# Half of one LayerNorm's transposes moved from TensorE to DMA, with the projection behind it regrouped

## The chip, the cores and the metric

The kernel runs on one core of a Trainium2 chip. The core has TensorE (PE: matrix products and, against an identity, transposes; both go to PSUM), VectorE (DVE), ScalarE (ACT), GpSimd (POOL) and a queue for transfers that SyncE (SP) issues. Each engine works off its own list of instructions in order. The metric is the device time of one execution in microseconds, the median of several.

## The reference, cut to what matters

One layer of a streaming encoder works on 256 tokens of 2048 features in float32. The part that matters here is the seam between its first feed-forward block and its mixer:

```
h = LN(alpha*h + 0.5*SwiGLU_1(h))                      # first FFN, then this LayerNorm
proj = h @ w_in                                        # one combined projection
qa, ka, va, q_lat, kv_lat, gates = split(proj)         # va: 1024 columns, gates: 4096
```

The LayerNorm takes mean and variance over the 2048 features of a token, and then a gain and a bias per feature. Two attentions, a cross attention and a second FFN follow.

## The kernel before, in words

**Operands.** Each float32 operand of a product is split into a rounded high part (hi, a copy by ACT) and the rest (lo, a subtraction by DVE). A product is three matmuls: hi by hi, lo of the activations by hi of the weights, and hi of the activations by lo of the weights. TensorE contracts over 128 features at a time, so 2048 features are 16 K tiles. Tokens come in two halves of 128 (`tt` 0 and 1).

**Weights.** Weights come from HBM in units of 2048 columns (1 MB) through three `raw` buffers, and are split into one of two `hi`/`lo` pairs or, where an item names tags, into free activation blocks. `add` appends an item (a function, the weights it needs, a count of weight pairs that are still held, a priority) to a list; `run` walks the list, loads and splits the weights of coming items as soon as a pair is free, and then calls the item. `weave` puts side steps ahead of the main items with given numbers. The order on each engine follows this program order, the priorities (SOON is 400, the default 0) and a compile-time estimate of when things are ready; `issue_after` pins one instruction behind another on its engine. `fetch` pins a weight load behind the transpose that was last sent before it in program order, and `send` pins a transposing transfer behind the last weight load; both are on SP.

**The LayerNorm.** At the end of the FFN, `out_proj` leaves 16 or fewer K tiles of its last column group as a skewed group: `skewed` first does four units for token half 0 and keeps their weights, and then the same four for token half 1. That lets the LayerNorm of half 0 run while TensorE still works on half 1. The next projection (A's values, `val`) is skewed in the same way, so that half 1 of the LayerNorm runs beside half 0 of the values. `ln_scale` makes mean and reciprocal root in a chain of small DVE operations. `ln_T` then takes quarters `q` of 512 features (4 K tiles): it normalises (DVE for even q, ACT for odd q), turns four 128x128 tiles on TensorE into one PSUM tile `at` (L421), applies gain and bias on the way out of PSUM (ACT L428 and DVE L430, in turns), and splits the result into hi (ACT L255) and lo (DVE L256) of the activations `T`. The transposes are pinned behind the matmul before them. Quarters 0 and 1 come ahead of the last of the four units of the other half, quarters 2 and 3 behind it.

**The values.** A's values are 1024 columns in two groups of 512. The first group's unit `g` holds K tiles 4g to 4g+3 of 512 columns, so all 16 K tiles are needed within the first four units (12 matmuls each and half). The second group follows with both halves together, 24 matmuls a unit. Each group takes two PSUM tiles of the pool `mm` (four buffers; the pool `at` has four, too). The four gate groups and the latent projection behind them take PSUM by turns: one pool for the plain products, the other for the products of sums (`mm_sums`), with the roles swapped from group to group. `forms_step` prepares sums of activations for these groups on DVE and ACT.

**Planes.** In other places the kernel already turns activations by DMA: `planes` copies float32 words on ACT as two planes of 16 bits (L846), `send` turns them by a transposing transfer on SP (L850), and `join` puts the words together again on ACT (L854). `turned_norm` does so with the LayerNorm behind the mixer: it normalises on DVE (L1405), sends, joins, applies gain and bias (ACT L1426 and DVE L1428, in turns) and splits.

## Time and profile before

| | us |
|---|---|
| median of three runs | 2433.39 (2433.3 to 2434.96) |
| profiled execution, its own time | 2432.52 |
| its span, first to last instruction | 2430.7 |
| TensorE busy in the span | 2422.3 |
| VectorE busy | 2130.9 |
| ScalarE busy | 1553.2 |

TensorE's granted clock is 1.0 throughout. The span is what lies between the first and the last instruction; the profiled execution's own time is 1.8 us more, and is 0.9 us below the median. In the views, "PE" rows are matmuls, "PEld" rows are the loads of the stationary operand, and an arrow with a name is what ended an idle time. The FFN's last matmuls lie at about 660 to 683 us of the span, the transposes of this LayerNorm between 680 and 697 us, and the values from 684 to 730 us.

### The profile page before, as it was taken

The numbers are of one execution on the slowest core, as the hardware profiler recorded it, in microseconds if no ns is written. First come the engines' busy times: TensorE is split into PE (matmuls) and PEld (weight loads), VectorE is DVE, ScalarE is ACT, GpSimd is POOL, SyncE is SP. The second block draws the span as 40 slices with busy tenths as digits, with TensorE's granted clock in tenths as the row PEclk, the third lists the DMA queues.
The fourth block names the chain that finished last, engine by engine and source line by source line (L and its number), as shares of the span: only waits on it lengthen the run. The fifth ranks groups of instructions, "written<-read, shape, count | busy, mean of one in ns | idle before, by whom it ended". The sixth has DMA issues, their size and how long they took to land.

```text
span 2430.7 us, 29702 instructions
## 1 busy us (share of the span) xinstructions
PE 2422.3 (100%) x11280; PEld 2022.8 (83%) x11280; DVE 2130.9 (88%) x2437; ACT 1553.2 (64%) x2022; POOL 35.9 (1%) x81
## 2 busy tenths in 40 slices
PE   9999999999999999999999999999999999999999
PEld 8888888888888888888888888888888888888887
DVE  8999989899889998779788889979879999888997
ACT  6676745666555557878565687765666675556662
POOL 0000000000000001000000000000000000000000
PEclk9999999999999999999999999999999999999999
DMA  7766656667656657776577577655556766666665
GB/s 268 252 212 214 207 200 222 210 201 219 224 176 215 216 195 248 229 210 176 183 246 256 167 241 213 220 181 192 190 199 214 229 221 210 220 207 207 200 220 182
DMA packets 176414, 516.20 MB, mean 212 GB/s; under 512 B 111728, under 2 KB 112496, under 8 KB 121104
## 3 DMA queue, kind: packets, MB, share of 16 engines
q1 hardware_dynamic: 170816, 495.83, 61.6%
q0 software_dynamic: 4592, 17.30, 2.2%
q8 instruction: 88, 1.44, 0.2%
q10 hardware_dynamic: 864, 1.18, 0.1%
q14 instruction: 54, 0.44, 0.1%
HBM read 485.30 MB, written 2.10 MB: 201 GB/s over the span
## 4 chain that ended last, share of the span: by engine, by line
PE 89%; DVE 4%; ACT 3%; DMA 1%; issue 1%; SPq 0%; DVEq 0%; ACTq 0%
PE at L311 24%; PE mm L311 23%; PE at L366 11%; PE mm L366 11%; PE mm L298 10%; PE mm L277 4%; PE mm L279 2%; DVE lo L267 2%; ACT hi L264 1%; PE at L1034 1%; PE at L1505 0%; PE at L277 0%; DMA raw<-w_xv 0%; PE at L1088 0%; ACT H L854 0%
## 5 line engine op out<-in xcount | busy, mean ns | idle before, releaser
L264 ACT CAST hi<-raw 128x1024 fp32r<-128x1024 f32 (+1 forms) x852 | 804.0, 981 | 458.0 <-PE at L311 150.1
L267 DVE TENSOR_TENSOR lo<-raw,hi 128x2048 fp32r<-128x2048 f32 (+1 forms) x427 | 902.0, 2114 | 134.8 <-ACT hi L264 129.0
L311 PE MATMUL mm<-hi,T 128*128 128x512 f32 (+1 forms) x1312 | 307.5, 384 | 0.8 <-DVE v L400 0.7
L311 PEld LDWEIGHTS mm<-hi,T 128*128 128x128 f32 x1312 | 244.5, 188 | 46.9 <-DVE v L400 1.1
L264 ACT CAST X<-H 128x1024 fp32r<-128x1024 f32 (+1 forms) x170 | 174.8, 1035 | 160.9 <-DVE H L248 119.9
L311 PE MATMUL at<-hi,T 128*128 128x512 f32 x1136 | 272.3, 390 | 0.0
L311 PEld LDWEIGHTS at<-hi,T 128*128 128x128 f32 x1136 | 213.3, 188 | 44.5
L267 DVE TENSOR_TENSOR X<-H,X 128x2048 fp32r<-128x2048 f32 (+1 forms) x85 | 191.4, 2252 | 64.7 <-ACT X L264 64.7
L311 PE MATMUL mm<-lo,T 128*128 128x512 f32 (+1 forms) x656 | 158.4, 383 | 0.0
L311 PE MATMUL at<-lo,T 128*128 128x512 f32 x568 | 141.0, 389 | 0.0
L311 PEld LDWEIGHTS mm<-lo,T 128*128 128x128 f32 x656 | 122.3, 188 | 22.4
L311 PE MATMUL at<-hi,H 128*128 128x512 f32 x560 | 133.8, 390 | 0.0
L311 PEld LDWEIGHTS at<-lo,T 128*128 128x128 f32 x568 | 106.7, 188 | 22.1
L311 PEld LDWEIGHTS at<-hi,H 128*128 128x128 f32 x560 | 105.0, 188 | 21.5
L250 DVE TENSOR_TENSOR H<-H,raw 128x512 f32<-128x512 f32 (+1 forms) x170 | 115.4, 679 | 2.2
L311 PE MATMUL mm<-hi,H 128*128 128x512 f32 x480 | 115.5, 392 | 0.1
L311 PEld LDWEIGHTS mm<-hi,H 128*128 128x128 f32 x480 | 89.6, 188 | 18.9 <-DVE w L684 0.5
L248 DVE TENSOR_TENSOR H<-raw 128x1024 f32<-128x1024 f32 (+1 forms) x85 | 102.1, 1201 | 0.6 <-DMA raw<-w_gate 0.4
L366 PE MATMUL mm<-X,X 128*128 128x512 f32 x342 | 91.4, 393 | 0.0
L264 ACT CAST X<-raw 128x1024 fp32r<-128x1024 f32 (+1 forms) x54 | 55.4, 1035 | 47.9 <-DVE raw L250 38.6
L366 PE MATMUL at<-X,X 128*128 128x512 f32 (+1 forms) x315 | 82.6, 386 | 0.7 <-ACT X L264 0.7
L854 ACT COPY w<-w 128x1024 uint16<-128x1024 uint16 (+1 forms) x60 | 75.7, 1275 | 1.4 <-DMA w<-w 1.4
(387 smaller groups left out, 4151.3 us busy)
## 6 DMA issues: line engine op xcount, KB each, us to landing
raw<-ffn_w_in SPq DMA_DIRECT2D x150, 1024.0 KB, 4.9
raw<-ffn_w_out SPq DMA_DIRECT2D x66, 1024.0 KB, 4.9
raw<-w_gate SPq DMA_DIRECT2D x32, 1024.0 KB, 4.8
raw<-ffn_w_out_r SPq DMA_DIRECT2D x16, 1024.0 KB, 4.9
raw<-w_qk SPq DMA_DIRECT2D x16, 1024.0 KB, 5.6
raw<-w_o_b SPq DMA_DIRECT2D x16, 1024.0 KB, 4.8
raw<-w_out SPq DMA_DIRECT2D x16, 1024.0 KB, 5.0
raw<-w_xk SPq DMA_DIRECT2D x16, 1024.0 KB, 5.4
```

Source lines behind the costliest of these rows:

```text
L248: self.nc.vector.tensor_tensor(two[0], two[1], raw[:, :m].unsqueeze(1).to_broadcast([P, 2, m]), ALU.add)
L250: self.nc.vector.tensor_tensor(t[:, a * m:a * m + m], t[:, b * m:b * m + m], raw[:, a * m:a * m + m], ALU.add)
L264: self.last_hi = self.nc.scalar.copy(hi[:, c:d], src[:, c:d])
L267: self.last_lo = self.nc.vector.tensor_tensor(lo[:, :n], src, hi[:, :n].bitcast(F32), ALU.subtract)
L277: self.nc.tensor.matmul(ps, hi[j], x.both(kt), start=(j == 0), stop=False)
L279: self.last_mm = self.nc.tensor.matmul(ps[:, :S], lo[j], x.at(0, kt), start=False, stop=(j == n - 1))
L298: self.last_mm = self.nc.tensor.matmul(ps, x.at(xi, kt)[:, tt * P:(tt + 1) * P], w[wi][:, j * 512 + c:j * 512 + c + m], start=(start and j ...
L311: self.last_mm = self.nc.tensor.matmul(ps[tt, g][:, :n], x.at(xi, kt)[:, tt * P:(tt + 1) * P], w[wi][:, c:c + n], start=first and j + wi + ...
L366: self.last_mm = self.nc.tensor.matmul(bank[:, :m], a[xi], v[wi][:, c * m:(c + 1) * m], start=own and first and wi + xi == 0, stop=own and ...
L854: self.nc.scalar.copy(self.words(u, n).rearrange("p (c k) -> p k c", k=2), self.words(s, n).rearrange("p (k c) -> p k c", k=2))
L1034: nc.tensor.matmul(ps[:, c0:c0 + nk], q[:, tt * P:(tt + 1) * P], k[:, :nk], start=(j == 0), stop=(j == len(parts) - 1))
```

## The change

Quarters 0 and 1 of this LayerNorm stay on TensorE (`near`, before the last unit of the other half, as before). Quarters 2 and 3 go by `planes`, `send` and `join`, through the blocks `F` and `X2`, for both token halves, with default priority. Their steps lie at the end of the FFN and at the items 0 to 8 of the values.

The values are read in another layout: a unit now holds one pair of K tiles of all 1024 columns (`_pairs`, `mm_pair`), so the eight units `k` go through the features in order. Units 0 to 3 (K tiles 0 to 7, quarters 0 and 1) are done by token halves, 12 matmuls each and half; units 4 to 7 (quarters 2 and 3) with both halves together, 24 each. All four PSUM tiles of `mm` are held to the end and copied out there by `values`, two by ACT and two by DVE. The gates, the latent projection and one small product behind it swap the two PSUM pools. The sums of activations for the gates keep their places in time (items 9 to 12).

```diff
-    def mm_pair(self, ps, w, n, x, kts, first, last):
+    def mm_pair(self, ps, w, n, x, kts, first, last, tts=(0, 1)):
...
-                for tt in range(2):
+                for tt in tts:
...
+    def skewed_pairs(self, src, ps, xT, side, tags):
+        kept = {}
+        def add(k, tts, tags=None, held=0, keep=False, again=False):
+            def fn(w=None):
+                if keep:
+                    kept[k] = w
+                w = kept.pop(k) if again else w
+                if k == 0:
+                    ps.update({(tt, g): self.group_tile(0) for tt in tts for g in range(2)})
+                self.mm_pair(ps, w, 512, xT(), (2 * k, 2 * k + 1), k == 0, k == 7, tts)
+            self.add(fn, *(() if again else ((src[:, k * 2048:(k + 1) * 2048], tags),)), held=held)
+        def build():
+            self.skewed(lambda tt, k, **kw: add(k, (tt,), **kw), (), tags)
+            for k in range(4, 8):
+                add(k, (0, 1))
+        self.weave(self.collect(build), side)
...
+        side = dict(steps(1))
+        for i, c in enumerate(SUMS_GATE):
+            side.setdefault(9 + i, []).append((self.forms_step(fx, SUMS_GATE, c, xT), 0))
+        side[12].insert(0, values)
+        self.skewed_pairs(t["w_va"][0], ps, xT, side, (None, None, ("H5", "H0", "early"), ("X0", "X1", "turned")))
...
-            self.pair_group(n % 2, t["w_gate"][n], 512, KT, xT, AT_GATE[n], fx, ps, qs, None, SUM_HOME + ("H5",),
+            self.pair_group(n % 2 ^ 1, t["w_gate"][n], 512, KT, xT, AT_GATE[n], fx, ps, qs, None, SUM_HOME + ("H5",),
...
-        self.pair_group(0, t["w_lat"][0], 512, KT, xT, SUMS_IN, fx, lps, lqs, None, SUM_HOME + ("H5",))
+        self.pair_group(1, t["w_lat"][0], 512, KT, xT, SUMS_IN, fx, lps, lqs, None, SUM_HOME + ("H5",))
...
-            ps = self.at_tile()
+            ps = self.mm_tile()
...
+        def near(tt):
...
+                self.ln_T(self.h[tt], got[tt], tt, ln, x["T"], (0, 1))
...
+        if not homes[0]:
+            def low(f, *a):
+                return f(*a), 0
+            side = {0: [scale(1), low(send, 0, 2), low(planes, 0, 3)], 1: [low(send, 0, 3)], 2: [low(join, 0, 2)],
+                    3: [near(1)], 4: [low(join, 0, 3), low(planes, 1, 2)], 5: [low(send, 1, 2), low(planes, 1, 3)],
+                    6: [low(send, 1, 3)], 7: [low(join, 1, 2)], 8: [low(join, 1, 3)]}
+            return lambda tt: side if tt else ([scale(0)], [near(0)], [low(planes, 0, 2)])
...
-        ln = [self.ln_steps(n, st, x) for n in ("ln_ffn1", "ln_mix", "ln_x")]
+        ln = [self.turned_norm("ln_ffn1", st, x, (None, None, "F", "X2")), None, self.ln_steps("ln_x", st, x)]
...
-    r["w_va"] = _tok(w[:, 2 * aw:3 * aw])
+    r["w_va"] = _pairs(*_halves(w[:, 2 * aw:3 * aw]), 512, [()])
```

47 lines of the change are left out of this document (16 added, 31 removed).

## The prediction

> **What bounds the kernel now.** I read the page first, then the waits of TensorE, then the seam by stages, along the chain of work, and in order of time.
>
> ```profile
> span 2430.7 us, 29702 instructions
> PE 2422.3 (100%) x11280; PEld 2022.8 (83%) x11280; DVE 2130.9 (88%) x2437; ACT 1553.2 (64%) x2022; POOL 35.9 (1%) x81
> PEclk9999999999999999999999999999999999999999
> ...
> PE at L493 <- DVE w L470: 1.1, 1, 1.1
> PE mm L311 <- DVE v L400: 0.7, 1, 0.7
> ```
>
> TensorE is busy for 2422.3 of 2430.7 us at full clock, and its longest waits for another engine are 1.1 and 0.7 us. So an edit gains only what it takes off TensorE's list, less the waits that this uncovers. The stages of the seam, each with the busy time of the engines:
>
> ```profile
> 684.04:692.52 8.48, 8.48 (x40) 6.80 (x39) 8.27 (x23) 6.09 (x11) 0.00 (x0) 1.00 0.00 0
> 692.52:696.95 4.43, 4.43 (x29) 3.87 (x28) 4.04 (x7) 3.52 (x8) 0.00 (x0) 1.00 0.48 150
> 696.95:707.93 10.98, 10.98 (x51) 9.10 (x50) 10.58 (x21) 7.21 (x12) 0.00 (x0) 1.00 0.32 109
> 707.93:729.69 21.76, 21.76 (x97) 18.02 (x96) 16.80 (x24) 10.98 (x16) 1.23 (x2) 1.00 0.61 212
> ```
>
> TensorE fills every stage. DVE is nearly full, too: 8.27 of 8.48 us and 10.58 of 10.98. ACT has 2.39, 0.91 and 3.77 us free in the first three stages, and 10.8 in the last. DMA is at 0.00 while half 0 of the values starts. The chain of work names the transposes:
>
> ```profile
> 680.29 1.04 PE at L421 x8
> ...
> 683.41 0.87 PE at L421 x8
> 684.28 8.40 PE mm L298 x36
> 692.68 0.87 PE at L421 x8
> ...
> 696.32 0.87 PE at L421 x8
> 697.20 32.66 PE mm L298 x144
> ```
>
> The four batches of eight transposes cost 1.04 us and three times 0.87. A matmul of 512 columns costs 32.66 / 144 = 0.2268 us, so a unit of 12 is 2.72 and one of 24 is 5.44.
>
> In order of time, the chain from transposes to the first value matmul, and then the second half's:
>
> ```profile
> 680.27 1.06 PE L421 MATMUL at<-ident,h 128*128 128x128 f32 x8
> 683.03 1.14 ACT L255 CAST T<-w 128x512 fp32r<-128x512 f32 x2
> 683.68 0.69 DVE L256 TENSOR_TENSOR T<-w,T 128x512 fp32r<-128x512 f32 x1 [0.34 <-ACT T L255]
> 684.04 2.28 PE L298 MATMUL mm<-hi,T 128*128 128x512 f32 x8
> 684.43 1.45 PEld L298 LDWEIGHTS mm<-hi,T 128*128 128x128 f32 x7 [0.22 <-DVE T L256]
> 690.64 1.52 ACT L415 ACTIVATE h<-h,nb,y 128x512 f32<-128x512 f32 x2 [1.90 <-DVE nb L403]
> 695.68 1.29 DVE L256 TENSOR_TENSOR T<-w,T 128x512 fp32r<-128x512 f32 x2 [0.24 <-ACT T L255]
> 696.95 2.07 PE L298 MATMUL mm<-hi,T 128*128 128x512 f32 x8
> ```
>
> This decides the first term. The transposes of half 0 start at 680.27. Quarter 0 is out of PSUM and rounded to hi from 683.03 on, and its lo ends at 683.68 + 0.69 = 684.37. The second matmul of the values reads that lo: it is the row at 684.43 with 0.22 us idle for it. TensorE already waits for the chain there, although the second batch of transposes lies between.
>
> **The change part by part.**
>
> *Transposes removed.* The second and the fourth batch go: 2 x 0.87 = -1.74 us on TensorE's list.
>
> *What comes back at half 0.* Without the second batch TensorE has its last FFN matmul out 0.87 us earlier, but the lo of quarter 0 still ends at 684.37, because the steps of that chain (transposes, four gains of each engine, hi, lo) are the same and start at the same row. The second matmul reads the lo first, in the pair layout as in the old. So +0.87: the whole batch turns into a wait. The bounds are 0, if DVE and ACT, with fewer gains to make around it, finish quarter 0 that much sooner, and 1.4, if a normalising for the planes (0.54, below) slips in front. I take 0.87, since the gains of quarters 2 and 3 lie behind this chain and not in it.
>
> *Half 1.* Three units follow, 8.2 us from the second matmul, and the transposes of half 1 stay at 692.5. After the unit of 2.72 us TensorE now arrives at 696.95 - 0.87 = 696.08, and its second matmul at 696.31. The lo of quarter 0 is the first of two in the row at 695.68, mean 0.645, so it ends between 696.33 and 696.4. That is a wait of 0.1. The bounds are 0, and 1.4 if one join's work on DVE (two gains and a lo, prices below) stands in front. I take 0.1: the near steps have the higher priority.
>
> *The detour by planes.* Four pieces (two quarters, two halves) each issue what the LayerNorm behind the mixer issues, whose rows are:
>
> ```profile
> L846 ACT COPY X<-h x4: 1038/1044/1046, 1383.9 to 1390.7; 128x1024 uint16<-128x1024 uint16 x4
> ...
> L854 ACT COPY X<-X x4: 1361/1368/1384, 1388.3 to 1407.6; 128x1024 uint16<-128x1024 uint16 x4
> ...
> L1426 ACT ACTIVATE X<-X,vecs x8: 480/504/517, 1389.7 to 1412.9; 128x128 f32<-128x128 f32 x8
> ...
> L1428 DVE TENSOR_SCALAR X<-X,vecs x8: 340/341/347, 1390.1 to 1410.3; 128x128 f32<-128x128 f32 x8
> ...
> L1405 DVE TENSOR_SCALAR h<-h,mv,y x8: 537/541/543, 1383.0 to 1393.7; 128x512 f32<-128x512 f32 x8
> ...
> L850 SPq DMA_TRANSPOSE X<-X x4: 1231/1232/3229, 1385.0 to 1391.9; - x4
> L850 SPq DMA_TRANSPOSE H<-H x12: 1231/1238/7732, 1250.0 to 1418.3; - x12
> ...
> raw<-w_va SPq DMA_DIRECT2D x8, 1024.0 KB, 5.7
> X<-X SPq DMA_TRANSPOSE x4, 4.6
> ```
>
> On ACT a piece is a planes copy 1.04, a join 1.36, two gains of 0.50 and a hi of 0.63: 4.0 us. On DVE it is a normalising 0.54, two gains of 0.34 and a lo of 0.69: 1.9. On SP it is one transfer that holds the queue for 1.23 and lands after 4.6. What it replaces, and what else stands on ACT there:
>
> ```profile
> L428 ACT ACTIVATE w<-at,vecs 128x128 f32<-128x128 f32 x16 | 6.8, 454 | 1.3 <-PE at L421 1.0
> L430 DVE TENSOR_SCALAR w<-at,vecs 128x128 f32<-128x128 f32 x16 | 6.3, 404 | 1.7 <-ACT w L428 1.6
> L255 ACT CAST T<-w 128x512 fp32r<-128x512 f32 x8 | 4.7, 619 | 0.8 <-DVE w L430 0.5
> L264 ACT CAST hi<-raw 128x1024 fp32r<-128x1024 f32 x11 | 11.1, 1052 | 9.0 <-issue 5.6 <-PE mm L298 3.4
> L891 DVE COPY H<-mm 128x512 f32<-128x512 f32 x2 | 1.4, 685 | 0.0
> L891 ACT COPY H<-mm 128x512 f32<-128x512 f32 x2 | 1.2, 577 | 0.2 <-PE mm L298 0.2
> ```
>
> Per piece ACT loses two gains of 0.45 and the hi of 0.62, and for quarter 3 a normalising of 0.8. So ACT has some 8.4 us more to do in all. DVE loses two gains of 0.40, the lo, and for quarter 2 a normalising that it does already: 0.6 more in all, which the free time of the last stage covers; without that cover it would be the 0.6. ACT's has to be followed by its deadline.
>
> The first unit that needs quarter 2 is k = 4. TensorE starts half 1 of unit 0 at 696.2, four units later it is 707.1, and the fifth matmul of unit 4 (four times 0.227 later, 708.0) is the first to read quarter 2 of half 1. From 684.2, where the two hi of quarters 0 and 1 end, ACT has in program order up to there: two hi of unit 3 (2.1), four planes (4.2), one normalising (0.8), four gains and two hi of half 1 (3.1), three pieces' joins with gains and hi (9.0), and the hi of units 4 and 5 (4.2). That is 23.3 us, so without one idle moment it ends at 707.5, and DVE's lo at 708.2, just as the sixth matmul reads it. ACT will not be free of idle: it waits in this stretch for DVE (1.90 in the row at 690.64) and for PSUM (1.0 in the L428 row). But two items on this list, the hi of unit 5 (due only at 712.5) and the planes of half 1's quarter 3, may fall behind. The bounds are 0 (these two, 3.1 us, come later) and 1.9 (worked out below). I take +0.5. The last piece is due with unit 6 at 718.0 and has ten more microseconds, with ACT half idle: nothing.
>
> *SP.* The first six loads of the values were issued by 677.6:
>
> ```profile
> 660.33 17.31 SPq L193 DMA_DIRECT2D raw<-w_va  x6
> ```
>
> Units 4 and 5 are the last two of these, and now stand behind the sends: unit 4's behind two, unit 5's behind the third, unit 6's behind the fourth. With ACT through the hi of unit 3 at 686.3, the planes end at 687.3 and 688.4, and two sends of 1.23 at 689.7; unit 4's load lands 5.7 later, at 695.4, and its buffer pair only comes free when the hi matmuls of unit 0 end, at 698. DMA stands at 0.00 before this, so that is the cover, 2.6 us wide for the start of the hi, and 10.6 for the last moment (707.1 less one cast of 1.05 and 5.7 of landing: issue by 700.3).
>
> *Values, pairs and PSUM.* 192 matmuls and eight loads of 1 MB remain; the pair order has the same forms. The four copies out of `mm` (0.58 and 0.69 each, two on either engine) come at the end. The gates start in `at`, which is free, and want `mm` only in their second unit, 5.44 us later; two copies behind one lo of 2.29 are done within 3.7. Nothing, and if that cover went, the excess over 5.44. The latent projection and the small product behind it swap pools with like distances: nothing. The sums for the gates keep their places, but may find DVE later; the last stage has 21.76 - 16.80 = 5 us of DVE free to take that.
>
> The sum is -1.74 + 0.87 + 0.1 + 0.5 = -0.27 us. The profiled execution, at 2432.52, would become 2432.25; it stands 0.87 below the median of the runs, so the forecast there is 2433.1.
>
> One rule of the Trainium skill prices the removed work otherwise. The page "TensorE: Matmul & The Clock Gate", section "Part 4: PE-mode transpose", gives about 275 ns for a 128x128 transpose within a kernel, and sixteen of those would be 4.4 us by that estimate. The duration of one agrees with this trace:
>
> ```profile
> L421 PE MATMUL at<-ident,h x64: 269/273/300, 680.3 to 1754.8; 128*128 128x128 f32 x64
> ```
>
> But eight of them pass in 0.87 us on the chain, 109 ns each, because they overlap; only that falls away.
>
> **The rivals.**
>
> *The removal pays in full.* Both batches come off and no wait follows: 2433.39 - 1.74 = 2431.65. For it: less work around the chain on both engines. Against it: the wait of 0.22 us that stands there now. Chance 0.18.
>
> *The join of quarter 2, half 1, comes late on ACT.* Its planes queue behind half 1's gains and hi (the second hi ends 0.62 behind the start of the row at 695.68) and run from 696.3 to 697.3; the third send goes out behind unit 4's load at 697.4, unit 5's load behind it at 698.6 and lands at 704.3, its hi takes ACT until 706.4, and then the join, two gains, hi and lo end at 710.1. The lo is due at 708.2: 1.9 late. The sum becomes -1.74 + 0.87 + 0.1 + 1.9 = +1.1, 2434.5. For it: ACT has nothing to spare by program order. Against: DVE has the mean and root of half 1 by 690.64, and TensorE's transposes come at 692.5 only, so ACT can make these planes between. Chance 0.20.
>
> *SP holds the weights back (slower).* All loads from unit 4 on are pinned behind sends. If a send holds the queue not 1.23 but 7.73 us, as the slowest of the rows above did, two of them put unit 4's load at 687.3 + 15.5 = 702.8; it lands at 708.5, its first cast ends at 709.6, and TensorE waits 2.5. Each of the next two loads stands behind one more such send (8.1 with its own issue, against 5.44 of TensorE's work), 2.6 each. Together 7.7, less the net 0.77 of the other terms: 2440.3. It decides from (700.3 - 687.3) / 2 = 6.5 us a send. For it: 7.73 was seen. Against: the medians are 1.23, and DMA is idle at that time. Chance 0.14.
>
> *Each removed transpose is worth its whole duration.* 16 x 0.273 = 4.4 us less, 2429.0; the 0.87 of the chain speaks against it. Chance 0.02.
>
> **How the numbers follow.** The forecast, 2433.1, has 0.43, and 0.03 is left for an order on the engines that I don't see. The range leaves out most of the SP rival, the whole-duration rival and the rest: 0.14 + 0.02 + 0.03 = 0.19. It goes from full removal in an execution like the profiled one (0.87 below the median), 2430.8, to a late join with both other upper bounds (1.3 more at half 1, 0.5 at half 0) in a run at the high end of those shown (1.57 above the median), 2437.9. About 0.2% (4.9 us) is what a measurement of this kernel can tell from no change. The forecast, full removal and late join all lie within that: 0.43 + 0.18 + 0.20 = 0.81, and with the whole-duration rival 0.83. Slower has the SP rival and a little of the rest, 0.15; faster 0.02, since nothing on the list is worth 4.9 us.
>
> **What the profile will show.** Right: 16 instead of 32 transposes in this seam, 0.87 us a batch; a wait of TensorE of about 0.9 us (0.5 for hi and 0.4 for lo, from ACT and DVE) ahead of the first two value matmuls; the first value matmul still near 684; the gates' first matmul near 729.4 instead of 729.69. ACT nearly full from 684 to 708; four sends of about 1.23 us on SP between 686 and 705, and unit 4's load landed by 698. Wrong: a wait of TensorE for `raw` loads or for `hi` at unit 4 or 5 (the SP rival), for T behind a join at unit 4 of more than 1 us (late join), or no wait at all at 683 (full removal). A wait for `mm` or `at` at the gates, or a shift of more than 3 us behind 735, would mean a cost that I have not listed.

## The result, and the profile after

The changed kernel takes 2438.07 us (median of 14 runs, 2435.84 to 2443.86); the kernel before took 2434.44 on the same chip (14 runs, 2432.79 to 2438.71). The ratio is 1.0018, 95% interval 1.0011 to 1.0025: 3.6 us slower, which is little, but the interval does not include 1. Forecast was 2433.1, no change. Of the 4.97 us between forecast and measurement 1.05 is the kernel before itself, which took 2433.39 in the runs that the forecast was made from. The profiled execution took 2439.88 us, 7.36 more than that of before. Three single executions of the experiments, of 2669.76 to 4077.75 us at clocks of 0.56 to 0.85, are left out of every median, excess and ratio below.

The page of the changed kernel (busy time, share, instructions; then the granted clock in 40 slices):

```profile
span 2438.1 us, 29690 instructions
PE 2421.9 (99%) x11264; PEld 2020.1 (83%) x11264; DVE 2132.0 (87%) x2439; ACT 1561.2 (64%) x2028; POOL 36.0 (1%) x81
PEclk9999999999999999999999999999999999999999
```

The 16 transposes are gone (11264 against 11280), TensorE's busy time is 0.4 us less, the span 7.4 us longer. So TensorE waits. What it waited for (total, times, longest; one row of 1.1, the same in the kernel before, is left out):

```profile
PE mm L278 <- ACT hi L265: 3.2, 1, 3.2
PE mm L312 <- ACT T L256: 2.1, 2, 1.1
PE mm L312 <- DVE v L401: 1.3, 1, 1.3
PE mm L367 <- DVE T L257: 1.2, 2, 0.8
...
PE mm L312 <- DVE T L257: 0.6, 2, 0.4
```

The second and the last row, T from ACT (L256) and, at L312, from DVE (L257), are the seam. The first row is elsewhere, near 1400. The third and the fourth lie behind the seam, too; they were 0.7 and 0.4 before and make up most of the rest, 1.4 us. That much is within what one kernel shows by itself: from the gates' first matmul to the end of the span the two traces of the kernel before take 1701.0 and 1704.4 us.

**The seam.** The same four stages as before (half 0's values, half 1's transposes and chain, and the rest up to the gates, cut once):

```profile
684.25:693.19 8.94, 8.58 (x36) 6.74 (x37) 7.10 (x18) 7.28 (x10) 0.00 (x0) 1.00 0.79 251
693.19:698.02 4.83, 3.77 (x22) 2.94 (x20) 3.78 (x11) 4.44 (x10) 0.00 (x0) 1.00 0.28 52
698.02:709.00 10.98, 10.76 (x46) 8.69 (x47) 8.56 (x13) 8.80 (x11) 0.00 (x0) 1.00 0.67 201
709.00:731.31 22.31, 22.31 (x100) 18.39 (x99) 19.73 (x32) 13.48 (x22) 1.23 (x2) 1.00 0.69 256
```

From the transposes at 680.12 to the first value matmul it takes 4.13 us (before 3.77, from 680.27 to 684.04), then 8.94 (8.48), 4.83 (4.43) and 33.29 (32.74): the seam is 51.19 us instead of 49.42. In the first and the third stretch one batch of eight transposes fewer stands (0.79 us each by the starts of the rows: 683.25 to 684.04 and 696.16 to 696.95), so the time that came in is 0.36 + 0.79 = 1.15 and 0.46 in half 0, and 0.40 + 0.79 = 1.19 and 0.55 in half 1. In order of time, all engines, cut to the rows that matter:

```profile
680.12 1.04 PE L422 MATMUL at<-ident,h 128*128 128x128 f32 x8
680.72 1.92 SPq L871 DMA_TRANSPOSE F<-F  x1
682.63 1.05 ACT L867 COPY X<-h 128x1024 uint16<-128x1024 uint16 x1
682.73 0.53 SPq L194 DMA_DIRECT2D raw<-w_va  x1
683.28 0.69 DVE L755 TENSOR_TENSOR h<-h,mm 128x512 f32<-128x512 f32 x1 [0.24 <-PE mm L299]
683.59 1.13 ACT L256 CAST T<-w 128x512 fp32r<-128x512 f32 x2
684.00 0.69 DVE L391 BATCH_NORM_STATS2 bn<-h 128x6 f32<-128x512 f32 x1
684.25 0.73 PE L312 MATMUL mm<-hi,T 128*128 128x512 f32 x2 [1.01 <-ACT T L256]
684.61 0.68 DVE L257 TENSOR_TENSOR T<-w,T 128x512 fp32r<-128x512 f32 x1
685.34 1.66 PE L312 MATMUL mm<-hi,T 128*128 128x512 f32 x6 [0.36 <-DVE T L257]
688.48 2.00 ACT L265 CAST X<-raw 128x1024 fp32r<-128x1024 f32 x2 [1.59 <-DMA raw<-w_va]
694.53 1.04 ACT L867 COPY F<-h 128x1024 uint16<-128x1024 uint16 x1
695.48 1.74 ACT L429 ACTIVATE w<-at,vecs 128x128 f32<-128x128 f32 x4
697.35 1.14 ACT L256 CAST T<-w 128x512 fp32r<-128x512 f32 x2
698.02 0.50 PE L312 MATMUL mm<-hi,T 128*128 128x512 f32 x1 [1.06 <-ACT T L256]
```

On ACT a planes copy (L867) runs at 682.63, and only behind it the hi casts that TensorE waits for, at 683.59. DVE puts the last addition to half 1's `h` (L755) and a piece of its statistics (L391), 0.69 us each, ahead of the lo as well. In half 1 the next planes copy stands at 694.53, ahead of the gains of the transposes that went out at 693.19. And unit 3's load, at 682.73 behind the first send, lands late: its casts stand at 688.48 on ACT after 1.59 us of waiting, with all of half 1 behind them. The chain of work that ended last runs through this load:

```profile
682.73 5.73 DMA raw<-w_va
...
688.48 2.01 ACT X L265 x2
```

**Near 1400.** The third and the fourth transposing transfer of the LayerNorm behind the mixer, then ACT's casts of the weights w_xk that are loaded between them, and TensorE's row, in the kernel before and in the changed one:

```profile
1390.01 1.23 SPq L850 DMA_TRANSPOSE X<-X  x1
1391.93 3.23 SPq L850 DMA_TRANSPOSE X<-X  x1
1395.08 2.00 ACT L264 CAST hi<-raw 128x1024 fp32r<-128x1024 f32 x2 [2.51 <-DMA raw<-w_xk]
1396.18 3.92 PE L277 MATMUL mm<-H,hi 128*128 128x512 f32 x16 [0.28 <-ACT hi L264]
```

```profile
1391.81 1.84 SPq L871 DMA_TRANSPOSE X<-X  x1
1395.36 4.50 SPq L871 DMA_TRANSPOSE X<-X  x1
1399.81 1.99 ACT L265 CAST hi<-raw 128x1024 fp32r<-128x1024 f32 x2 [5.44 <-DMA raw<-w_xk]
1400.90 5.51 PE L278 MATMUL mm<-H,hi 128*128 128x512 f32 x16 [3.21 <-ACT hi L265]
```

Measured from the third transfer, a load lands some 3 us later: the casts come 8.00 us behind its issue instead of 5.07. TensorE waits 3.21 us instead of 0.28, and its next 16 matmuls take 5.51 us instead of 3.92. That is 2.9 + 1.6 of the 7.36 us, 700 us behind the change. None of the instructions there was edited. Up to that place TensorE's list is 16 transposes shorter, SP has four transfers more, and the lists of ACT and DVE are longer by six and two instructions.

### The profile page after: what moved, and what is told of

It is laid out like the page before. It is cut to its first block, busy times and chain, and to the rows that moved or that the text cites. A ratio compares the mean times of both kernels' runs of the same rounds, so it can differ in the third digit from the quotient of the medians.

```text
span 2438.1 us, 29690 instructions
## 1 busy us (share of the span) xinstructions
PE 2421.9 (99%) x11264; PEld 2020.1 (83%) x11264; DVE 2132.0 (87%) x2439; ACT 1561.2 (64%) x2028; POOL 36.0 (1%) x81
## 3 DMA queue, kind: packets, MB, share of 16 engines
q8 instruction: 88, 1.44, 0.2%
## 4 chain that ended last, share of the span: by engine, by line
PE 92%; DVE 3%; DMA 2%; ACT 2%; issue 1%; SPq 0%; DVEq 0%; ACTq 0%
PE at L312 26%; PE mm L312 24%; PE mm L367 11%; PE at L367 11%; PE mm L299 9%; PE mm L278 5%; PE mm L280 2%; PE at L1038 1%; DVE lo L268 1%; PE at L278 1%; ACT hi L265 1%; DMA raw<-w_xv 1%; PE at L1523 0%; PE at L1092 0%; PE at L280 0%
## 5 line engine op out<-in xcount | busy, mean ns | idle before, releaser
L312 PE MATMUL mm<-hi,T 128*128 128x512 f32 (+1 forms) x1328 | 312.1, 383 | 4.6 <-ACT T L256 2.1
L312 PE MATMUL at<-hi,T 128*128 128x512 f32 x1216 | 291.2, 389 | 0.0
L312 PEld LDWEIGHTS mm<-hi,T 128*128 128x128 f32 x1328 | 246.7, 188 | 53.1 <-ACT T L256 2.9
L312 PEld LDWEIGHTS at<-hi,T 128*128 128x128 f32 x1216 | 228.2, 188 | 47.7
L312 PE MATMUL mm<-lo,T 128*128 128x512 f32 (+1 forms) x664 | 161.2, 382 | 0.0
L312 PE MATMUL at<-lo,T 128*128 128x512 f32 x608 | 150.3, 389 | 0.0
L312 PEld LDWEIGHTS mm<-lo,T 128*128 128x128 f32 x664 | 123.7, 188 | 22.8
L312 PEld LDWEIGHTS at<-lo,T 128*128 128x128 f32 x608 | 114.1, 188 | 23.7
L312 PE MATMUL at<-hi,H 128*128 128x512 f32 x560 | 133.7, 389 | 0.0
L312 PEld LDWEIGHTS at<-hi,H 128*128 128x128 f32 x560 | 104.9, 188 | 21.6
L312 PE MATMUL mm<-hi,H 128*128 128x512 f32 x480 | 115.5, 391 | 0.0
L312 PEld LDWEIGHTS mm<-hi,H 128*128 128x128 f32 x480 | 89.5, 188 | 19.0 <-DVE w L685 0.5
L367 PEld LDWEIGHTS mm<-X,X 128*128 128x128 f32 x360 | 66.8, 188 | 15.9 <-DVE X L268 2.2
L367 PE MATMUL at<-X,X 128*128 128x512 f32 (+1 forms) x297 | 77.7, 385 | 0.4 <-ACT X L265 0.4
```

Of the source, the lines that this page charges most:

```text
L312: self.last_mm = self.nc.tensor.matmul(ps[tt, g][:, :n], x.at(xi, kt)[:, tt * P:(tt + 1) * P], w[wi][:, c:c + n], start=first and j + wi + ...
L367: self.last_mm = self.nc.tensor.matmul(bank[:, :m], a[xi], v[wi][:, c * m:(c + 1) * m], start=own and first and wi + xi == 0, stop=own and ...
```

## The experiments

"Seam" is the time from the transposes of half 0 to the gates' first matmul in the profiled execution (kernel before: 49.42). Excess is the median less that of the kernel before, measured together with it. The cuts of code are shortened to what a run changes at this LayerNorm, with "..." where something is left out.

**The change and the kernel before again**, unaltered.

> The changed kernel once more, for a second profile. Its first one lost 1.6 us in the seam (gates' first matmul 731.31 against 729.69 of before) and 5.2 us more near 1400 us, in the LayerNorm behind the mixer, where TensorE waited 3.2 us for hi of w_xk and the next sixteen matmuls took 5.51 us instead of 3.82. Theory A (order on ACT): the loss of the seam is in the order of the engines' lists and comes again: gates at 731.0 to 731.6. Theory B (landing): the loss near 1400 is a spread of transfers in an unchanged part and is mostly gone this time: the waits from 1350 to 1450 under 1.5 us, execution at about 2436. Rival C (the change reaches that far): the waits near 1400 are 3 us or more again.

Measured: 2436.60, excess 2.95, ratio 1.0015 (1.0006 to 1.0024); seam 51.75, waits for T of 1.45 and 1.34 us; near 1400 only 0.3.

> The kernel before once more, for a second profile. Its first one waited 0.3 us between 1350 and 1450. Theory B: that number spreads from execution to execution, from 0.3 to some 3 us, and the seam is as it was (gates' first matmul 729.5 to 729.9). Rival C: it is 0.3 us again, and the seam the same; ratio 1.000 within 0.001 by either.

Measured: 2433.17, ratio 0.9999 (0.9990 to 1.0008); seam 49.45, near 1400 a wait of 0.71. The changed kernel's waits in the seam recur, its loss near 1400 does not in this execution.

**The regrouping alone**: all quarters turned by TensorE in their old places.

```
-        ln = [self.turned_norm("ln_ffn1", st, x, (None, None, "F", "X2")), None, ...]
+        near = self.ln_steps("ln_ffn1", st, x)
+        ln = [lambda tt: dict(zip((0, 3, 4), near(tt))) if tt else near(tt), None, ...]
```

> The regrouping alone: values in K-tile pairs, gates and latent projection in the other PSUM pools, but all four quarters of the LayerNorm turned on TensorE, at their old places. Theory A: the regrouping costs nothing, the four batches of 0.87 us stand as before, gates' first matmul at 729.5 to 729.9, time within 0.6 us of before. Rival (the regrouping costs): gates later than 730.5 or new waits for PSUM, and more than 1.5 us on the time.

Measured: 2433.10, ratio 0.9999 (0.9990 to 1.0008), seam 49.16. Pairs, token halves and the other PSUM cost nothing that can be told, within about 2 us by the interval, and nothing in the trace's seam.

**Planes behind the near chain**: three of the four planes copies stand behind the hi casts of their half.

```
-                with self.tc.issue_after(self.next_hi.ins):
+                with self.tc.issue_after(self.next_hi.ins if homes[0] or (tt, q) == (0, 2) else self.ln_act.ins):
                     self.planes(hs, e[q][:, tt, 0, :], 512)
```

> The change, with three of the four planes copies on ACT pinned behind the hi copies of quarters 0 and 1 of the same half (one plane of half 0, both of half 1), so that they can't stand in front of the steps that TensorE waits for. Theory A: the wait at half 0 falls from 1.9 to about 1.0 us, that at half 1 from 1.8 to 0.3, the gates start near 729.0, and the time is 2.3 us less than the changed kernel's. Rival (transfers): the waits stay, because a load or a landing is late, and the time stays at 2437 to 2438. Rival (late join): the waits move to unit 4 of the values, 1 to 3 us.

```profile
683.12 2.39 PE L312 MATMUL mm<-hi,T 128*128 128x512 f32 x8
696.74 2.38 PE L312 MATMUL mm<-hi,T 128*128 128x512 f32 x8 [1.24 <-ACT T L256]
```

Measured: 2436.03, excess 2.4, ratio 1.0009 (1.0000 to 1.0018), seam 49.87. The wait of half 0 is gone with the copy ahead of it, more than the expectation had said (about 1.0 us left). Half 1's stays, against the 0.3 expected: from its transposes to its first value matmul it takes 5.04 us, 4.83 in the changed kernel. There the late load is still ahead; ACT waits 1.12 us for it.

**And unit 3's load ahead of the first send** (the send one step later).

```
-  side = {0: [scale(1), low(send, 0, 2), low(planes, 0, 3)], 1: [low(send, 0, 3)], ...
+  side = {0: [scale(1), low(planes, 0, 3)], 1: [low(send, 0, 2), low(send, 0, 3)], ...
```

> The planes of half 0's quarter 3 and of half 1 stand behind the hi casts that release the value matmuls (as in planes_behind), and the first send stands behind unit 3's load of weights instead of ahead of it. Order theory (A): in half 1 the wait for T (1.06 and 0.22 us in the changed kernel, 1.24 with the planes behind alone) has its second cause in that load, so it falls to 0.3 us or less, the hi of unit 3 starts near 684 instead of 688, and the gates' first matmul is at 728.6 to 729.2 against 729.8 with the planes behind alone and 731.3 in the changed kernel. If the seam is all there is, the time is 1.5 to 3 us under the changed kernel's. Rival (C, a loss behind the seam): the gates' matmul moves as said, but the time stays 1.5 us or more above the kernel before, because the time from the gates' first matmul to the last one is longer than the 1696.6 to 1699.9 us of the kernel before.

Measured: 2435.86, excess 2.9, 1.0010 (1.0001 to 1.0019); the gates' first matmul at 729.31, not at the 728.6 to 729.2 expected, and the seam 49.66. The casts of unit 3 came at 684.85, and half 1's stretch from transposes to first value matmul fell from 5.04 to 4.17 us. But on ACT and DVE a join and two normalisings for the planes stood ahead of half 1's gains, and a wait for T of 0.40 us was left. Half 0 had one of 0.74: the one planes copy that was not moved came at 680.03 here, 0.4 us behind the start of the transposes, and its gains behind it. The time stayed where it was: the seam is not all.

**No transfers**: the planes are written where the joins read, so quarters 2 and 3 are not transposed.

```
-  self.planes(hs, e[q][:, tt, 0, :], 512)
+  self.planes(hs, e[q][:, tt, 1, :], 512)          # and no send
```

> The changed kernel without its four transposing transfers: the planes are written where the joins read, so the transposition of quarters 2 and 3 is left out of what is computed, and every instruction of ACT, DVE and TensorE stays. No load of weights stands behind a send any more. Order theory (A): the wait for T of half 0 stays (1.0 us, the planes copy ahead of the hi casts is still there), half 1's is smaller by what unit 3's load cost, gates' first matmul 730 to 731. Rival (C, transfers cost behind the seam): the time falls by more than the seam's gain, to within 1 us of the kernel before plus the seam's rest. If the time stays where the changed kernel's is, transfers have no part in it.

```profile
681.55 1.05 ACT L867 COPY F<-h 128x1024 uint16<-128x1024 uint16 x1
682.62 1.35 ACT L875 COPY F<-F 128x1024 uint16<-128x1024 uint16 x1
685.99 1.04 ACT L867 COPY X<-h 128x1024 uint16<-128x1024 uint16 x1
686.92 1.15 ACT L256 CAST T<-w 128x512 fp32r<-128x512 f32 x2
687.60 2.40 PE L312 MATMUL mm<-hi,T 128*128 128x512 f32 x8 [3.31 <-ACT T L256]
```

Measured: 2440.13, excess 7.2, 1.0031 (1.0019 to 1.0043), the slowest of all; seam 51.50. With nothing to land first, the list takes a join (L875) and its gains ahead of the hi casts too, and the wait is 3.31 us instead of the 1.0 expected. So the order on ACT makes such a wait without any transfer. It does not show where all of the 7.2 us come from: the profiled execution took 2435.77, 4.4 less than the median, and ran at full clock, while the other five show mean clocks of 0.998 or 0.999.

**Transfers alone**, then **twice as many**: the regrouping alone, with transposing transfers of zeros that nobody reads.

```
+  self.nc.gpsimd.memset(e[q][:, :, 0, :], 0.0)      # once for each of quarters 2 and 3
...
+  with self.tc.issue_after(self.last_load.ins):     # steps 0, 1, 5, 6; twice in eight_transfers
+      self.sent = self.send(v[:, 1, :], v[:, 0, :], 512)
```

> The regrouping alone (all quarters turned by TensorE, as in pairs_only, gates at 729.16) with four transposing transfers of zeros issued on SP at the change's places; nobody reads them, GpSimd fills their sources. Order theory (A): the seam costs at most what unit 3's late load costs, 0 to 0.6 us, and the time is pairs_only's within 1 us (2432 to 2434.5). Rival (C): transfers on SP cost behind the seam whatever is computed: the time is 1.5 us or more above pairs_only's, with the gates' first matmul in place.

> As transfers_alone (which stood 1.15 us above the kernel before), with each of the four transfers issued twice. Rival (C, transfers on SP cost time by themselves, outside the seam): the excess doubles, 2.3 us or more above the kernel before, with the seam at its 49.2 to 49.8. If transfers cost nothing by themselves: within 1.2 us of the kernel before.

Measured: four 2434.12, excess 1.15, 1.0006 (0.9997 to 1.0014), seam 49.45; eight 2433.97, excess 0.6, 1.0001 (0.9991 to 1.0010), seam 49.42. Doubling adds nothing that can be told. A limit of this test: with no planes to wait for, the transfers went out earlier than in the change, the first of the four at 664.88.

**The activations' lo last** in unit 0, on top of planes_and_load.

```
-  for wi in range(2):  ...  for xi in range(2 - wi):
+  for wi, xis in ((0, (0,)), (1, (0,)), (0, (1,))):  ...  for xi in xis:
```

> As planes_and_load, and in unit 0 of the values the products with the lo of the activations come last instead of second, so TensorE starts on hi and on the weights' lo while DVE makes the activations' lo. Order theory (A): what is left of the waits for T in both halves (lo on DVE, 0.2 to 0.4 us each) goes as well, gates' first matmul 0.3 to 0.8 us ahead of planes_and_load's, near 728.2, 1.5 us ahead of the kernel before; time 2431.5 to 2433 if nothing behind the seam takes it back. Rival (C): the gates' matmul moves as said and the time stays above the kernel before.

```profile
710.86 2.34 PE L312 MATMUL mm<-hi,T 128*128 128x512 f32 x9 [1.21 <-DVE T L257]
```

Measured: 2435.17, excess 2.2, 1.0012 (1.0003 to 1.0020), seam 50.05 instead of the 48.9 to 49.4 expected. The T of half 1's quarter 2, due with unit 4, came 1.21 us late. On ACT its hi cast (707.78) stood behind the casts of unit 5's weights (705.88), and those waited 1.76 us for a load that SP had issued behind the third send. In planes_and_load the same hi cast (703.62) came ahead of these weights (704.93). That is the late join of the prediction's rivals, seen here only.

**A wait by itself**: the kernel before with four, then eight, gains made again on ACT ahead of the first hi cast.

```
+  if ln == "ln_ffn1" and tt == 0 and q == 0:
+      for j in (0, 2) * 2:                          # * 4 in delay_3_2
+          nc.scalar.activation(v[:, j, :], ps[:, j * P:(j + 1) * P], AF.Identity, ...)
```

> The kernel before with four more gains on ACT (values that stand there already, made again) ahead of the first hi cast of half 0: at about 0.41 us each in a row the first value matmul comes 1.6 us later, less what it waited already. Theory that only the length of a wait counts: the seam from the transposes to the gates grows from 49.4 to 50.5 to 51.0 and the time by the same 1.1 to 1.6 us, to about 2434.3. Rival (D, a wait of TensorE costs more than its length, because the clock it is granted falls in some executions): the time grows by 1 us or more beyond that, runs spread to 2437 and more, and some show a mean clock of 0.999 or less.

> The same with eight more gains, 3.2 us, and one or two other instructions that the list takes in between: a wait of TensorE of 3.2 to 4.2 us ahead of the first value matmul. Length alone: the time grows by 3.2 to 4.2 us, to 2436.2 to 2437.2. Rival (D): it grows by 5 us or more, to 2438 to 2441, with mean clocks of 0.998 to 0.999 in most runs, as in the kernel without transfers, whose one wait was 3.3 us and whose median stood 7.2 us above the kernel before.

```profile
686.23 0.49 PE L298 MATMUL mm<-hi,T 128*128 128x512 f32 x1 [2.70 <-ACT T L255]
689.10 1.91 PE L298 MATMUL mm<-lo,T 128*128 128x512 f32 x4
693.02 1.07 PE L298 MATMUL mm<-lo,T 128*128 128x512 f32 x4
```

Measured: four 2436.34, excess 2.95, 1.0012 (1.0003 to 1.0020), seam 50.90; eight 2438.14, excess 4.75, 1.0022 (1.0013 to 1.0030), seam 54.26. With eight the wait is 2.70 us, not 3.2 or more. After it four matmuls take 1.91 us at 689.10 and 1.07 at 693.02, and the stretch to half 1's transposes is 10.42 us instead of 8.48. The mean clock is 0.99 from 686.2 to 688.2, 0.50 from 688.2 to 691.6, and 1.00 again behind that. So this wait cost 1.9 us more than itself. With four gains the trace's seam is 1.5 longer, the median 2.95, and the interval holds both; the profiled execution (2433.66) is the fastest of its run, so its trace does not show what the others lost.

**Near first**: on top of planes_and_load, half 1's normalisings for the planes behind the lo, and the join of half 0's quarter 3 behind half 1's hi. Run twice.

```
+  with self.tc.issue_after(self.ln_lo.ins):
       nc.vector.tensor_scalar(hs, hs, mean, r, ALU.subtract, ALU.mult)
-  self.join(v[:, 1, :], v[:, 0, :], 512)
+  self.join(v[:, 1, :], v[:, 0, :], 512, self.ln_act if (tt, q) == (0, 3) else None)
```

> As planes_and_load, and in half 1 the normalising for the planes on DVE stands behind the lo casts of the values, and the join of half 0's quarter 3 behind the hi casts of half 1, so nothing of the detour stands ahead of the chain in either half. Order theory: the stretch from half 1's transposes to its first value matmul falls from 4.17 us to 3.6 to 3.9, the seam from 49.66 to about 48.9 to 49.3, at most 0.5 us under the kernel before, because in half 0 the removed batch lay under the chain anyway. Time 2432.5 to 2434 if the seam is what counts; 2435 or more if the excess of the detour kernels has another cause than waits in the seam.

> The same kernel as near_first. By theory E again 0.5 to 1 us above the kernel before, with clocks of 0.999 in half of the runs; seam near 48.3 us in its trace if no send is slow in it, and if the trace is of a slow execution, a wait of TensorE for hi or T at the values of units 4 to 7 behind a send of over 3 us, or a wait elsewhere that the other theories name.

```profile
683.23 2.40 PE L312 MATMUL mm<-hi,T 128*128 128x512 f32 x8
692.48 1.83 ACT L429 ACTIVATE w<-at,vecs 128x128 f32<-128x128 f32 x4 [2.51 <-PE at L422]
695.49 2.15 PE L312 MATMUL mm<-hi,T 128*128 128x512 f32 x8
```

Measured: 2434.11 and 2435.43, excess 0.7 and 1.9, 1.0005 (0.9996 to 1.0014) and 1.0009 (1.0001 to 1.0018); seams 48.29 and 48.46, with no wait of TensorE over 0.32 in the seam. In half 1 ACT stands idle until the transposes come, and the removal pays: the first trace's seam is 1.1 us under the kernel before, more than the 0.5 expected, 0.4 of it in half 0 and 0.7 in half 1. The medians are not under it. Both profiled executions (2432.45 and 2433.03) are the fastest of their runs, so the traces don't show what the medians lost.

**Weights first**: near_first with unit 5's load ahead of the third send, the sends later, and the join of half 0's quarter 3 moved to step 8.

```
-  1: [low(send, 0, 2), low(send, 0, 3)], ... 4: [low(join, 0, 3), ...], 5: [low(send, 1, 2), low(planes, 1, 3)],
-  6: [low(send, 1, 3)], ... 8: [low(join, 1, 3)]
+  2: [low(send, 0, 2), low(send, 0, 3)], ... 5: [low(planes, 1, 3)], 6: [low(send, 1, 2), low(send, 1, 3)], ...
+  8: [low(join, 0, 3), low(join, 1, 3)]
```

> As near_first, with the sends one or two steps later, so that unit 5's load of weights stands ahead of the third send instead of behind it (near_first: issued at 699.97 and landed at 705.35, against 677.32 in the kernel before), and the join of half 0's quarter 3 behind everything that is due sooner. Theory (E: the excess of near_first over its trace, 1.8 us, comes from executions in which a send holds SP for longer or lands later and the weights come late): the spread shrinks to the kernel before's 3 us, mean clocks are 1.000, and the median is 0.5 to 1.1 us under the kernel before, with the gates' first matmul about 48.3 us behind the transposes. If the excess has another cause: median 0.5 to 1 us above the kernel before again, clocks of 0.999 in half of the runs.

Measured: 2436.07, excess 2.5, 1.0011 (1.0002 to 1.0020), seam 49.84, not the 48.3 expected: half 0 has a wait of 0.75 us, with the gains behind the one planes copy that was not moved (680.16), as in planes_and_load. Near 1400 there is a wait of 3.34 us. Unit 5's load came early (issued at 686.43 with unit 4's), yet neither spread nor median fell. So these loads are not what costs the excess, or not alone.

**The change a third time.**

> The changed kernel once more: 2 to 4 us above the kernel before. Seam 51.2 to 51.8 us with waits of TensorE for T of 2 to 3 us in sum in both halves; behind the seam, either a loss near 1400 as in the first trace (a wait of 3.2 us for hi and 16 matmuls at a clock of 0.66, when transposing transfers landed late) or none, as in the second. If each trace shows waits in the seam and the clock falls behind them in some (0.9 or less in a window of 10 us), the clock is the rest of the loss.

```profile
1400.00:1405.00 5.00, 5.00 (x13) 3.84 (x13) 3.57 (x5) 5.00 (x9) 0.00 (x0) 0.50 1.00 369
```

Measured: 2437.99, excess 4.45, 1.0016 (1.0007 to 1.0025); seam 50.31, under the 51.2 to 51.8 expected, with waits for T of 1.74 us in sum instead of 2 to 3; near 1400 a wait of 2.81 us, then (the row; the column behind POOL's is the clock) five microseconds at a clock of 0.50.

**The count of TensorE's instructions.** The third transposing transfer near 1390 held SP for 1.23 or 1.24 us in all seven traces with 11280 matmuls so far, whatever else they did, and for 1.45 to 2.76 in all ten with 11264. One packet of code (16 KB) moves with it. It lies in the three microseconds ahead of that transfer in the kernel before, and in the three behind its issue in the changed one (queue: packets, MB, share; the queue of the other transfers is left out):

```profile
q8 instruction: 1, 0.02, 1.9%
```

```profile
q8 instruction: 1, 0.02, 2.4%
```

This queue moves 88 packets, 1.44 MB, in either kernel. That fits TensorE's 22,560 matmuls and weight loads at 64 bytes each, 256 to a packet, so the queue is taken to be TensorE's code. If so, sixteen matmuls fewer put every later packet sixteen matmuls later in the work. Three runs test that. The first two give the 16 back as eight tiny f32 matmuls, of two instructions each, ahead of the transposes that are left.

```
+  for j in range(2 if ln == "ln_ffn1" else 0):
+      nc.tensor.matmul(ps[:, :8], h[:, 4 * q * P:(4 * q + 1) * P], self.ident[:, :8], start=True, stop=True)
```

> near_first with eight tiny matmuls of eight f32 columns (two instructions each, results written over at once) ahead of the four groups of transposes that are left, so that TensorE's list has 11280 matmuls again. Theory F: the code packet lies 2.5 to 3.0 us ahead of the third transfer near 1390, that transfer holds SP for 1.23 us, TensorE's wait for hi there is 0.2 to 0.7 us; the runs are as close together as the kernel before's and the median is 0.3 to 1.1 us under it (seam 48.3 us and up to 0.6 for the tiny ones). If the count has no part: hold 1.45 to 2.8, median 0.7 to 2 us above the kernel before, as near_first.

> The changed kernel with the same eight tiny matmuls. Theory F: the loss in the seam stays (gates' first matmul 51 to 52 us behind the transposes), the hold near 1390 is 1.23 us, and the median is 1.5 to 2.5 us above the kernel before instead of 3.3 to 4.9. If the count has no part: 3 to 5 us above, hold 1.45 to 2.8.

The third takes 16 others away from the regrouping alone.

```
-  for wi in range(2):
+  for wi in range(2 - less):                        # less: the last two units of the values
```

> The regrouping alone (pairs_only), with the 16 products of the weights' lo in the last two units of the values left out: that part of the first FFN's values is not computed. TensorE's list is 16 matmuls and 16 weight loads shorter, as in the changed kernel, and no engine does anything of the detour. By the work left out (16 x 0.227 = 3.6 us) and the 0.3 of pairs_only it would be 3.9 us under the kernel before. Theory F: the code packet lies at the issue of the third transfer near 1390, which holds SP for 1.45 to 2.8 us, and the median is only 1 to 2.5 us under the kernel before, with a spread of 5 us or more and mean clocks of 0.999 in some runs. If the count has no part: hold 1.23 and the full 3.6 to 3.9.

The third transfer in count_kept, with the start of its transposes, and then in sixteen_fewer with TensorE's row:

```profile
682.00 0.58 PE L421 MATMUL at<-ident,h 128*128 128x8 f32 x4 [1.99 <-issue]
1391.81 1.23 SPq L873 DMA_TRANSPOSE X<-X  x1
```

```profile
1389.55 3.26 SPq L871 DMA_TRANSPOSE X<-X  x1
1398.72 5.54 PE L278 MATMUL mm<-H,hi 128*128 128x512 f32 x16 [3.28 <-ACT hi L265]
```

Measured: sixteen_fewer 2436.09, excess 2.6, 1.0009 (1.0000 to 1.0018), with 3.6 us of matmuls left out and a seam of 45.81; it has nothing of the detour, its code packet lies within 0.5 us of the transfer's issue, and its trace has the hold, the wait of 3.28 us and 16 matmuls in 5.54. count_kept 2435.36, excess 1.8, 1.0006 (0.9997 to 1.0014), seam 49.56; changed_count_kept 2436.47, excess 2.9, 1.0011 (1.0002 to 1.0019), seam 50.28. Both hold 1.23 us, with the packet about 2.5 us ahead and waits of 0.25 and 0.33 us near 1400.

So the count decides where the packet falls, in both directions, and the hold follows it: the packet starts 2.1 to 2.6 us ahead of the transfer in all nine traces with 11280 matmuls, and within 0.3 us of its issue in all eleven with 11264. The second transfer, under way at that moment, parts them as cleanly. It lands 3.0 to 3.1 us behind its own issue in the nine, and 4.4 to 4.8 in the eleven.

What TensorE loses is another matter. It goes with the landing of the third transfer, not with its hold. In four traces, all with 11264 matmuls, that transfer lands after 8.7 to 9.2 us, and TensorE waits 2.81 to 3.34 us. In lo_last it lands after 7.2, and the wait is 1.30. In the other fifteen it lands after 6.0 to 6.5, and the wait is 0.71 at most, although the hold is 2.12 in near_first and 2.35 in no_transfers. Four of eleven against none of nine would come about by chance in some 7 of 100 cases if the count had no part in the loss. So that the count brings the loss near 1400 is likely, not shown.

The medians fit the count only in part. The expectation for count_kept, 0.3 to 1.1 us under the kernel before, failed: 1.8 above lies in the range set down for a count without a part. changed_count_kept, at 2.9, lies between the two ranges, and its seam stayed below the 51 to 52 expected, because on ACT the second planes copy (683.60) now stood behind the first hi cast (683.08). sixteen_fewer is 6.2 us above what the work left out would give, more than expected. Its trace has, besides the 3.28 and 1.6 us near 1400, three waits of 1.55 us in sum between 798 and 836, and even its fastest execution (2434.71) is 4.8 above that mark.

The tiny matmuls cost 0.36 us for each of the four groups, not the 0.6 in all that was expected, so count_kept could hardly come out under the kernel before. Its excess and that of changed_count_kept are still 1.7 and 2.1 us above their seams (0.14 and 0.86 over 49.42), which the intervals allow to be nothing. In count_kept 1.99 us of idle time stand ahead of the transposes; in the other traces it is 0 to 1.25 at this place, of either kind of kernel. The trace shows where it comes from: ACT's first casts of the values' weights wait 3.41 us for a load (1.29 in near_first), DVE works behind them, and half 0 is normalised from 681.35 on instead of 678.70. Why the load comes late there was not tried. The remainder of the medians is open.

## Why the prediction was wrong, by its steps

- **Transposes removed, -1.74**: nearly right in size; each of the two batches is 0.79 by the starts of the rows, 1.58 in all. In near_first 1.1 of it reaches the gates.
- **Half 0, +0.87**: wrong; 1.15 + 0.46 = 1.61, above the upper bound of 1.4. That bound named the mechanism, but with a normalising of 0.54; what slipped in front was a planes copy of 1.05 on ACT, and the last addition and statistics of half 1 on DVE. planes_behind shows the copy as the cause. The premise, that the chain to the lo of quarter 0 takes as long as before, nearly held once nothing stood in front: in near_first this lo ends 3.89 us behind the start of the transposes (before 4.10), and half 0 keeps 0.41 of its 0.79.
- **Half 1, +0.1**: wrong; 1.19 + 0.55 = 1.74, above 1.4. One failing sentence is "the near steps have the higher priority". The order on an engine is a fixed list, made from estimated times: in the changed kernel a join, its gains and a planes copy, all of low priority, stand ahead of half 1's gains on ACT. The other cause is unit 3's load. With the copies behind the chain half 1's stretch stays at 5.04 us, with the load ahead of the first send it is 4.17, and with join and normalisings behind as well, in near_first, 3.64 (4.43 before): 0.7 of the batch's 0.79 then reaches the gates.
- **The join at unit 4, +0.5**: nothing in the changed kernel. The late join appeared in lo_last alone.
- **SP at nothing**: the price was near (sends held 1.24 to 1.92 us), the place was not. Unit 3's load, not unit 4's, was the first behind a send; the prediction had taken the first six loads as issued by then. TensorE did not wait for it, but ACT did, 1.59 us, with half 1's work behind. The rival of held weights did not occur in the seam.
- **Regrouping and PSUM at nothing**: right (pairs_only), as far as 2 us can be told.
- **The gates' first matmul at 729.4**: 731.31. The sum of the seam was -0.27 and is -1.58 + 1.61 + 1.74 = +1.77.
- **What the sum lacked**: anything behind the seam. The seam's 1.77 is about half of the 3.6 us by which the median grew. The prediction said that a shift of more than 3 us behind 735 would mean a cost not listed; the first and the third trace of the change show one, 2.5 to 2.9 us of wait more than before and then a lower clock. sixteen_fewer shows the same loss without the detour, so it needs nothing of it but the shorter list; that the shorter list is its cause is likely, as said above. What the other executions lose behind the seam stays open.

The Trainium skill, page "Runtime: NRT & Kernel Launch", section "Instruction fetch mechanics", has code arriving in blocks of 16 KiB, 256 instructions, and calls a crossing mostly hidden. The 88 packets agree with the size. For TensorE's own issue "hidden" agrees with the trace, too: in the kernel before, over 88 packets, it is busy for 2422.3 of 2430.7 us. The transfer that such a packet meets is held up all the same (1.45 us and more against 1.23). The page "TensorE: Matmul & The Clock Gate", Part 1, halves the clock after an idle window of some 3.4 us for about as long, an estimate of 1.7 us lost. The trace agrees on the loss (5.51 - 3.92 = 1.59) and on the half (0.50), but not on the length: waits of 2.70 and 2.81 us were enough, and two of 3.31 and 3.34 had no such effect.

That the code packet at that place holds the transfer up is shown by its position and the hold going together in 20 traces, with the count changed in both directions. By which path 16 KB does so was not tried. No version was faster than the kernel before by more than its interval; pairs_only, 0.55 us under it, has no transposes removed.

## What to carry to other kernels

Work taken off the bounding engine is worth what is left after the chain that feeds it, so look first at what the other engines' lists will hold ahead of that chain, and at which loads will stand behind a new transfer. Here a low priority didn't put ready work behind the chain, an explicit order did. A change of a few instructions moved the code packets of the rest of the program here, so compare traces far behind the change, and test by taking the same number of instructions away elsewhere. A wait of nearly 3 us cost TensorE over half as much again by the clock in four of six cases. A trace shows one execution: see first where it lies among the times of its run.

## What the runs showed of the hardware

- After a wait of 2.7 to 3.3 us TensorE ran slower in four of six such traces: mean clocks of 0.50 to 0.84 over 5 us, 1.6 to 1.9 us lost where it was read from rows, and up to 2.8 (16 matmuls in 6.71 us instead of 3.92 in changed_third). After 3.31 us in no_transfers and 3.34 in weights_first it ran on at full clock. In delay_3_2 the clock fell 2 us after TensorE had started again, and was 0.50 for 3.4 us.
- The third transposing transfer near 1390 holds SP for 1.23 or 1.24 us in nine traces and, with a code packet at its issue, for 1.45 to 3.26 in eleven. The one before it lands 3.0 to 3.1 or 4.4 to 4.8 us behind its issue. Without such a packet holds can be long, too: the fourth one holds 3.23 us in the kernel before.
- An f32 matmul of eight columns counts as two matmuls and two weight loads (11264 and eight of them give 11280), and passes in 0.18 us (0.36 for two, from one group's start to the transposes behind it).
